# A hybrid decoder layer with routed experts: expert 1's low parts, the slot tables and the finishing of places, moved

## The chip, the cores and the metric

The kernel runs on one core of one Trainium2 chip. The metric is the device time of one execution in microseconds (us); of a kernel the median over its runs is given.

## The reference

Sixteen learned rows are put ahead of 2048 tokens of width 1024, and one decoder layer is computed: a projection, a pooling mixer and gated linear attention, an output projection added to the input, a router, and sixteen experts of which each token visits two. The last step is a final norm. What matters here is the router and the experts:

```python
def hier_moe(x, w_rg, b_rg, w_re, b_re, w_gate, w_up, w_down):
    ...
    g_sel = jnp.argmax(g_logits, axis=-1)
    p_g = jnp.take_along_axis(g_prob, g_sel[:, None], axis=-1)
    ...
    top_p, top_i = lax.top_k(e_prob, TOP_K_IN_GROUP)
    top_p = top_p / jnp.sum(top_p, axis=-1, keepdims=True)
    weights = p_g * top_p
    expert_id = g_sel[:, None] * EXPERTS_PER_GROUP + top_i
    combine = jnp.sum(jax.nn.one_hot(expert_id, N_EXPERTS, dtype=f32) * weights[..., None], axis=1)
    y = jnp.zeros(xf.shape, f32)
    for e in range(N_EXPERTS):
        h = jax.nn.silu(xt @ w_gate[e]) * (xt @ w_up[e])
        y = y + combine[:, e:e + 1] * (h @ w_down[e]).astype(f32)
```

Everything is float32; an expert has 256 hidden columns.

## The kernel before, in words

Tokens go in 16 tiles of 128 rows. Every float32 product is made of three matmuls, high by high, low by high and high by low, so each operand is split: ScalarE writes the rounded high part (L111 for weights, L107 for tokens), and VectorE or GpSimd the rest as the low part (L112, L108).

**Routing.** `route_pick` (L583) finds the two experts of each token of a tile and writes a 0/1 matrix `A` (L615). `route_rest` (from L620) turns it into slots: tiny matmuls with a matrix of ones (`ones_b`) and a triangular one (`before_b`) count the tokens that came before (L645, L647), VectorE computes slot numbers from the counts (L662 to L676, `ix` is the result), and GpSimd writes a record per token and expert into the table in HBM through an indirect DMA (L690). For the last tile two more tiny matmuls (L641, L642) and an addition (L643) give the total of each expert. `rank_experts` (L708) sorts the experts by their totals.

**Places.** The sixteen experts are then worked off in sixteen places; the first two places hold experts 0 and 1, the others hold experts by rank. A place has up to 320 slots, in row groups j = 0, 1, 2 of 128, 128 and 64 rows (the last six places only 0 and 1). For a place the kernel loads the slot table's columns into SBUF (`load_places`, L1105, by SyncE), sets the words of tokens' first and second visit (`fix_words`, seven VectorE operations, L1115 to L1121), gathers the tokens' rows (`xg`, `xs`, indirect DMAs of GpSimd, all in the helper on L924), transposes them on TensorE (L946) with the split behind it (L107 on ScalarE, L108 on VectorE), and does the gate and up products. For places 0 and 1 these are `gate_rows` (L995 to L997, one row group at a time, since routing isn't finished when they start); later `gate_up` (L975 to L977). Then come `hidden`, the down products (`down`, L1036 to L1041), and their evacuation with the routing weight (L1052 on ScalarE, L1054 on VectorE) into a row tile `xr`, of which six form a ring.

**What a token's two visits need.** A place scatters its rows into a buffer `oe` in HBM, then gathers from `oe` what an earlier place has left for its tokens, adding it (`xr<-oe`). `square` (L1072, ScalarE) sums the squares, and `finish` scales the finished rows (L1078, three operations for three row groups) and scatters them into the output (`out_dram<-xr`). `finish(e-1)` stands behind `down(e)` for most places, so these scatters follow place e's scatters and gathers on GpSimd's queue.

**Weights.** Chunks of 128x1024 come through SyncE into buffers `raw` (three) and `wr` (two), in order; a buffer is free when both halves of its split are done. Expert 1's four chunks (`wb` 0 to 3) are split while the last tile is routed, with their low parts on GpSimd.

**What sets the order.** A tile scheduler places instructions by priority and dependence when the program is built; each engine then runs its own in that order. `must_follow` adds an order that the data don't ask for. Around the change these are: the counts of the last tile behind a given matmul of expert 0's `gate_rows` (`picked`, `gate_ops`), and expert 1's splits. Rows of TensorE are in this order: expert 0's row groups 0 and 2, expert 1's row groups 0 and 2 (banks `sp` and `o`), expert 0's and 1's row group 1, whose tokens are known only after routing.

Of the kernel before, what the change touches and what calls it, by code (L numbers as in the profile page):

```python
# [12 lines left out]
OP = mybir.AluOpType  # L13
# [4 lines left out]
NT = 16  # L18
# [52 lines left out]
def body(ctx, tc, I, O):  # L71
# [16 lines left out]
    def must_follow(ins, earlier):  # L88
        for o_ in earlier:
            tc.add_manual_dep(ins.ins, o_.ins.name,  # L90
                              mybir.DependencyInfo(mybir.DependencyClass.Sync, mybir.DependencyReason.DATA),
                              reason="rows written through indices")
# [527 lines left out]
    def route_rest(t):  # L620

        T = lambda n, w, dt=F32: wk.tile([128, w], dt, name=n)
        lg, r, gm, m1, m2, Ef, A, xn = OUT.pop(t)
        i = t - 1
        rc = rec[t % 3]
        rf = rc.bitcast(F32)
        sv = sv_all[:, i, :]
        first = t <= EARLY
        pp = bank("m2", (128, 2, 16))
        if t == EARLY + 1:  # L630
            nc.tensor.matmul(pp[:, 1], ones_b, acc[i % 2], start=True, stop=True)
            early = pp[:, 1]
            V.tensor_copy(counts, early)
            for row, at in ((late1, 128.0), (late2, float(SMALL)), (late3, float(CAP))):
                V.tensor_scalar(row[:, FIXED:], early[:, FIXED:], -1.0, at, op0=OP.mult, op1=OP.add)
            V.tensor_scalar(late2[:, :FIXED], early[:, :FIXED], -1.0, float(CAP), op0=OP.mult, op1=OP.add)
            V.tensor_scalar(late2[:, :FIXED], late2[:, :FIXED], 128.0, None, op0=OP.min)
            V.tensor_copy(late3[:, :FIXED], late2[:, :FIXED])
            V.scalar_tensor_tensor(late0[:, FIXED:], early[:, FIXED:], 48.0, iota16[:, FIXED:], op0=OP.mult, op1=OP.add)
        elif t == NT:  # L640
            nc.tensor.matmul(pp[:, 1], ones_b, acc[i % 2], start=True, stop=False)  # L641
            nc.tensor.matmul(pp[:, 1], ones_b, A, start=False, stop=True)  # L642
            V.tensor_tensor(counts, pp[:, 1], counts, op=OP.add)  # L643
        pp = pp[:, 0]
        picked[0] = nc.tensor.matmul(pp, before_b, A, start=True, stop=(t == EARLY + 1))  # L645
        if t != EARLY + 1:
            nc.tensor.matmul(pp, ones_b, acc[i % 2], start=False, stop=True)  # L647
        ngm, eg, sg, nm1, p2, den, w = T("ngm", 1), T("eg", 4), T("sg", 1), T("nm1", 1), T("p2", 1), T("den", 1), T("w", 2)
        V.tensor_scalar(ngm, gm, -1.0, None, op0=OP.mult)
        nc.scalar.activation(eg, lg[:, 0:4], AF.Exp, bias=ngm, accum_out=sg)  # L650
        V.tensor_scalar(nm1, m1, -1.0, None, op0=OP.mult)
        nc.scalar.activation(p2, m2, AF.Exp, bias=nm1)
        v16, t1, t2, tmp, vv = T("v16", 16), T("t1", 16), T("t2", 16), T("tmp", 16), T("vv", 2)
        lev = T("lev", 16)
        if first:
            V.scalar_tensor_tensor(v16, pp, 48.0, iota16, op0=OP.mult, op1=OP.add)
            V.scalar_tensor_tensor(t1, pp, 128.0, step1, op0=OP.is_ge, op1=OP.mult)
            V.tensor_tensor(lev, pp, from2, op=OP.is_ge)
            V.tensor_tensor(t2, lev, step2, op=OP.mult)
            V.scalar_tensor_tensor(lev, pp, float(CAP), lev, op0=OP.is_ge, op1=OP.add)  # L660
        else:
            V.tensor_tensor(v16, pp, per_slot, op=OP.mult)  # L662
            V.tensor_tensor(v16, v16, late0, op=OP.add)
            V.tensor_tensor(t1, pp, late1, op=OP.is_ge)
            V.tensor_tensor(t1, t1, step1, op=OP.mult)
            V.tensor_tensor(lev, pp, late2, op=OP.is_ge)
            V.tensor_tensor(t2, lev, late_step2, op=OP.mult)
            V.tensor_tensor(tmp, pp, late3, op=OP.is_ge)
            V.tensor_tensor(lev, lev, tmp, op=OP.add)
        V.tensor_add(v16, v16, t1)  # L670
        V.tensor_add(v16, v16, t2)
        for j in range(2):
            V.scalar_tensor_tensor(tmp, Ef[:, j], 1.0, v16, op0=OP.mult, op1=OP.mult, accum_out=vv[:, j:j + 1])
            V.scalar_tensor_tensor(tmp, Ef[:, j], 1.0, iota16, op0=OP.mult, op1=OP.mult, accum_out=sv[:, j:j + 1])
        ix = T("ix", 2, I32)
        last = V.tensor_copy(ix, vv)  # L676
        V.scalar_tensor_tensor(den, p2, 1.0, sg, op0=OP.add, op1=OP.mult)
        V.reciprocal(w[:, 0:1], den)
        V.tensor_mul(w[:, 1:2], w[:, 0:1], p2)
        tok = tok_all[:, i:i + 1]  # L680
        V.tensor_copy(rc[:, :, 0], tok.to_broadcast([128, 2]))
        V.tensor_scalar(rf[:, :, 6], tok.to_broadcast([128, 2]), OOB, None, op0=OP.add)
        for j in range(2):
            V.tensor_copy(rf[:, j, 5:6], sv[:, 1 - j:2 - j])
        V.tensor_scalar(rf[:, :, 3], w, r, None, op0=OP.mult)
        r2 = T("r2", 1)
        V.tensor_mul(r2, r, r)
        V.tensor_scalar(rf[:, :, 4], r2.to_broadcast([128, 2]), EPS * SCALE, None, op0=OP.mult)
        for j in range(2):
            s_ = nc.gpsimd.indirect_dma_start(  # L690
                out=table, out_offset=bass.IndirectOffsetOnAxis(ap=ix[:, j:j + 1], axis=0),
                in_=rc[:, j, :], in_offset=None, bounds_check=6143, oob_is_err=False)
            for o_ in table_ops:
                tc.declare_no_dep(s_.ins, o_.ins, reason="other slots")
            table_ops.append(s_)
        oe_ops.append((-1, nc.gpsimd.dma_start(oe[i * 128:t * 128, :], xn)))
        if t == EARLY + 1:
            V.tensor_copy(acc[(i + 1) % 2], A)
        elif t < NT:
            V.tensor_tensor(acc[(i + 1) % 2], acc[i % 2], A, op=OP.add)  # L700
        V.tensor_copy(sv[:, 2:4], w)
        for j in range(2):
            V.scalar_tensor_tensor(tmp, Ef[:, j], 1.0, lev, op0=OP.mult, op1=OP.mult, accum_out=sv[:, 4 + 3 * j:5 + 3 * j])  # L703
        V.tensor_copy(sv[:, 5:6], rf[:, 0, 4:5])
        V.tensor_copy(sv[:, 6:7], r)
        return last
# [197 lines left out]
    with ExitStack() as c2:  # L904
# [230 lines left out]
            for k in range(KB):  # L1135
                transposes(0, k, (0, 2), added[0])
        early = [gate_rows(0, 0, "mm"), gate_rows(0, 2, "mm", lambda k: k < 6 or transposes(1, k - 6, (0, 2)))]
        must_follow(picked[0], [gate_ops[2]])
        for k in range(4):
            split_chunk(nc.gpsimd)  # L1140
            load_chunks(min(8 + k, 10))
        for k in range(2, KB):
            transposes(1, k, (0, 2))
        load_places(0, FIXED, slice(0, FIXED))
        fix_words(0, FIXED, iota16)
        for e in range(FIXED, NE):
            load_places(e, e + 1, expert(e))
        first_rows = [ind(XG[e][1], hn_dram, col(e, 1, 0), False) for e in range(2)]
        gather(2)
# [15 lines left out]
                    transposes(0, i, (1,))  # L1165

        early_1 = [gate_rows(1, 0, "sp"), gate_rows(1, 2, "o", early_rest)]
        down(0, (0, 2))
        for e in range(NE):
            def between(i):  # L1170
                if e + 1 < NE and i % 2 == 0:
                    for k in range(i, i + 2):
                        transposes(e + 1, k, None if e else (1,))
                if e == 0:
                    if i in (2, 6):
                        fix_words(*((2, 9) if i == 2 else (9, 16)), place)
                    if i == 0:
                        for op in load_chunks(10 + WRB, mk):
                            must_follow(op, first_rows)
                else:  # L1180
                    if done[0] < len(stream) and (i < 2 if e == NE - 1 else i in (0, 1, 2, 3, 4, 6)):
                        gate = stream[done[0]][0] == "g"
                        for op in split_chunk():
                            if gate:
                                must_follow(op, hidden_done)
                        load_chunks(done[0] + WRB, mk)
                if e >= NE - 2 and i == 1:
                    RT[e] = [row_tile(True) for j in JS[e]]
                    for j in JS[e]:
                        add_oe(e, ind(RT[e][j][:rows[j]], oe, col(e, j, 0), False), True)  # L1190
# [16 lines left out]
            if e > 1:  # L1207
                for j in JS[e - 1]:
                    square(e - 1, j)
            if e == NE - 2:  # L1210
                finish(e - 1)
            down(e, None if e else (1,))
            if 1 < e < NE - 2:
                finish(e - 1)
            if e == 8:
                count_left(mk)

# [132 lines left out]
```

## Time and profile before

| what | value |
|---|---|
| median of 3 runs | 1127.05 us (1126.39 to 1127.88) |
| the profiled execution's own time | 1121.29 us |
| its span, first to last instruction | 1119.5 us |
| mean granted TensorE clock | 0.982 |
| TensorE busy | 1055.8 us, 94% |
| VectorE busy | 779.8 us, 70% |
| ScalarE busy | 565.7 us, 51% |
| GpSimd busy | 313.8 us, 28% |

Rows name an engine (PE is TensorE, DVE VectorE, ACT ScalarE, POOL GpSimd, SP SyncE), a line of the kernel, the operation and the tiles it writes and reads. In brackets stands how long the engine had been idle and what it waited for last. The clock is a share of TensorE's full rate.

### The profile page before, as it was taken

Reading aid. Unit: us, or ns where it says so; the run is one execution under the profiler, and the core shown is the slowest. Engines: PE = TensorE matmul, PEld = TensorE weight load, DVE = VectorE, ACT = ScalarE, POOL = GpSimd, SP = SyncE. Lnnn points to the kernel's source line nnn. Section 1 sums busy time; section 2 is a strip of 40 time slices with the busy share of each in tenths; the row PEclk is TensorE's granted clock in tenths of the full one; section 3 lists DMA queues with packets and bytes.
Section 4 is the critical chain, followed back from the end, with each engine's and each line's share of the span. In section 5 each row is a group of like instructions: output and inputs, shape, how many; then the busy total and the mean of one; then the engine's idle time right before and its main releaser. Section 6 shows DMA issues by size and latency. Waiting matters only on the chain. (4 is left out here: it accounts for less than half of the span.)

```text
span 1119.5 us, 19115 instructions
## 1 busy us (share of the span) xinstructions
PE 1055.8 (94%) x6614; PEld 946.5 (85%) x6614; DVE 779.8 (70%) x2649; ACT 565.7 (51%) x1192; POOL 313.8 (28%) x276
## 2 busy tenths in 40 slices
PE   7999999999999999999999998879999999989982
PEld 5888888888888889999999998558998899988861
DVE  6476666545555776878777788747787788867873
ACT  7545444334433643333333334337767777667741
POOL 2000000000000000121111105524677777776551
PEclk9999999999999999999999999989999999989996
DMA  8412332111121352533434344488888997889852
GB/s 279 166 66 76 107 101 90 62 57 48 67 85 57 115 196 67 170 142 120 145 124 151 114 153 160 132 235 237 221 248 230 242 264 214 231 256 311 255 152 74
DMA packets 64471, 174.09 MB, mean 156 GB/s; under 512 B 21012, under 2 KB 21317, under 8 KB 64368
## 3 DMA queue, kind: packets, MB, share of 16 engines
q1 hardware_dynamic: 36272, 105.72, 27.7%
q0 software_dynamic: 25504, 58.53, 20.0%
q10 hardware_dynamic: 2592, 8.55, 2.1%
q8 instruction: 54, 0.88, 0.3%
q14 instruction: 49, 0.40, 0.1%
HBM read 143.74 MB, written 57.74 MB: 180 GB/s over the span
## 5 line engine op out<-in xcount | busy, mean ns | idle before, releaser
L441 POOL DMA_DIRECT2D y_dram<-y x16 | 8.6, 541 | 391.2 <-DVE y L439 391.2
L924 POOL DMA_INDIRECT oe<-xr,tab x40 | 69.3, 1732 | 69.0 <-ACT xr L1052 57.3
L321 PE MATMUL mm<-wb,XL 128*128 128x512 f32 (+1 forms) x240 | 83.6, 348 | 0.0
L322 PE MATMUL mm<-wb,XH 128*128 128x512 f32 (+1 forms) x240 | 83.0, 346 | 0.0
L690 POOL DMA_INDIRECT table<-rec,ix x32 | 33.3, 1042 | 176.8 <-DVE tmp L703 85.4
L320 PE MATMUL mm<-wb,XH 128*128 128x512 f32 (+1 forms) x240 | 82.2, 342 | 0.0
L924 POOL DMA_INDIRECT xr<-oe,tab x39 | 75.4, 1932 | 17.8 <-issue 9.8
L523 PE MATMUL mm<-XL,ws 128*128 128x256 f32 (+1 forms) x256 | 73.0, 285 | 0.2 <-DVE XL L112 0.2
L522 PE MATMUL mm<-XH,ws 128*128 128x256 f32 (+1 forms) x256 | 73.0, 286 | 0.0
L524 PE MATMUL mm<-XH,ws 128*128 128x256 f32 (+1 forms) x256 | 72.2, 282 | 0.0
L111 ACT ACTIVATE XH<-xt 128x1024 fp32r<-128x1024 f32 x32 | 33.8, 1058 | 56.4 <-PE mm L524 36.0
L924 POOL DMA_INDIRECT out_dram<-xr,tab x39 | 55.6, 1426 | 20.8 <-DVE sr_y L60 7.4
L975 PE MATMUL mm<-xh,ws 128*128 128x320 f32 (+1 forms) x168 | 51.3, 306 | 0.0
L976 PE MATMUL mm<-xl,ws 128*128 128x320 f32 (+1 forms) x168 | 51.2, 305 | 0.0
L977 PE MATMUL mm<-xh,ws 128*128 128x320 f32 (+1 forms) x168 | 51.0, 304 | 0.0
L320 PE MATMUL mm<-ws,XH 128*128 128x512 f32 x112 | 47.4, 423 | 2.0 <-ACT XH L111 2.0
L321 PEld LDWEIGHTS mm<-wb,XL 128*128 128x128 f32 x240 | 45.4, 189 | 4.4
L1078 DVE SCALAR_TENSOR_TENSOR xr<-xr,sr_y,fw 128x1024 f32<-128x1024 f32 (+1 forms) x39 | 48.7, 1278 | 0.5
L320 PEld LDWEIGHTS mm<-wb,XH 128*128 128x128 f32 x240 | 45.1, 188 | 4.6
L322 PEld LDWEIGHTS mm<-wb,XH 128*128 128x128 f32 x240 | 45.1, 188 | 4.5
L523 PEld LDWEIGHTS mm<-XL,ws 128*128 128x128 f32 x256 | 48.1, 188 | 0.7 <-DVE XL L112 0.4
L524 PEld LDWEIGHTS mm<-XH,ws 128*128 128x128 f32 x256 | 48.4, 189 | 0.3 <-issue 0.2
(654 smaller groups left out, 3840.8 us busy)
## 6 DMA issues: line engine op xcount, KB each, us to landing
raw<-in_wgu_e_dram SPq DMA_DIRECT2D x42, 512.0 KB, 5.2
xt<-in_xT_dram SPq DMA_DIRECT2D x32, 512.0 KB, 3.5
xn<-in_xn_dram SPq DMA_DIRECT2D x32, 512.0 KB, 3.5
wr<-in_wgu_e_dram SPq DMA_DIRECT2D x22, 512.0 KB, 5.9
raw<-in_wd_e_dram SPq DMA_DIRECT2D x20, 512.0 KB, 5.6
hn_dram<-xn ACTq DMA_DIRECT2D x16, 512.0 KB, 3.3
oe<-xn POOLq DMA_DIRECT2D x16, 512.0 KB, 3.7
wr<-in_wd_e_dram SPq DMA_DIRECT2D x12, 512.0 KB, 5.8
```

What stands on the lines that cost most here:

```text
L111: return (nc.scalar.activation(hi, src, AF.Copy), (eng or V).tensor_tensor(lo, src, hi.bitcast(F32), op=OP.subtract))
L320: nc.tensor.matmul(q, xh[:, k, :], wh[:, c0:c1_], start=(k == 0), stop=False)
L321: nc.tensor.matmul(q, xl[:, k, :], wh[:, c0:c1_], start=False, stop=False)
L322: nc.tensor.matmul(q, xh[:, k, :], wl[:, c0:c1_], start=False, stop=(k == KB - 1))
L522: nc.tensor.matmul(ps[:, b], WS[k][0][:, c], XH[:, k, o:], start=(k == 0), stop=False)
L523: nc.tensor.matmul(ps[:, b], WS[k][0][:, c], XL[:, k, o:], start=False, stop=False)
L524: nc.tensor.matmul(ps[:, b], WS[k][1][:, c], XH[:, k, o:], start=False, stop=(k == KB - 1))
L924: return nc.gpsimd.indirect_dma_start(out=out_, out_offset=off if scatter else None, in_=in_, in_offset=None if scatter else off, bounds_c ...
L975: nc.tensor.matmul(p[:, c0:c1_], wh, xh, start=(k == 0), stop=False)
L976: nc.tensor.matmul(p[:, c0:c1_], wh, xl, start=False, stop=False)
L977: nc.tensor.matmul(p[:, c0:c1_], wl, xh, start=False, stop=(k == KB - 1))
L1078: V.scalar_tensor_tensor(x[:n], x[:n], r[:n], fw[:n], op0=OP.mult, op1=OP.mult)
```

## The change

Four things are changed.

1. For the last tile, `route_rest` puts the two `before_b`/`ones_b` matmuls first and the two that make the totals behind them; all four now follow the matmul of k = 6 of expert 0's row group 2 instead of k = 2.
2. The low parts of expert 1's four chunks go from GpSimd to VectorE, and each must follow the cast to `ix` of the last tile.
3. Of the table loads, those of places 0 to 4 remain ahead of the first gathers; those of 5 to 8 are made in place 0's products and those of 9 to 15 in place 1's. The fix of places 0 and 1 stands behind expert 1's early rows, that of places 2 to 8 goes from place 0's products to place 1's, that of 9 to 15 from place 0's to place 2's.
4. `finish(e-1)` stands ahead of `down(e)` for all places, where it stood behind it for places 2 to 13.

```diff
--- before.py
+++ after.py
@@ -637,14 +637,14 @@
             V.tensor_scalar(late2[:, :FIXED], late2[:, :FIXED], 128.0, None, op0=OP.min)
             V.tensor_copy(late3[:, :FIXED], late2[:, :FIXED])
             V.scalar_tensor_tensor(late0[:, FIXED:], early[:, FIXED:], 48.0, iota16[:, FIXED:], op0=OP.mult, op1=OP.add)
-        elif t == NT:
-            nc.tensor.matmul(pp[:, 1], ones_b, acc[i % 2], start=True, stop=False)
-            nc.tensor.matmul(pp[:, 1], ones_b, A, start=False, stop=True)
-            V.tensor_tensor(counts, pp[:, 1], counts, op=OP.add)
-        pp = pp[:, 0]
+        total, pp = pp[:, 1], pp[:, 0]
         picked[0] = nc.tensor.matmul(pp, before_b, A, start=True, stop=(t == EARLY + 1))
         if t != EARLY + 1:
             nc.tensor.matmul(pp, ones_b, acc[i % 2], start=False, stop=True)
+        if t == NT:
+            nc.tensor.matmul(total, ones_b, acc[i % 2], start=True, stop=False)
+            nc.tensor.matmul(total, ones_b, A, start=False, stop=True)
+            V.tensor_tensor(counts, total, counts, op=OP.add)
         ngm, eg, sg, nm1, p2, den, w = T("ngm", 1), T("eg", 4), T("sg", 1), T("nm1", 1), T("p2", 1), T("den", 1), T("w", 2)
         V.tensor_scalar(ngm, gm, -1.0, None, op0=OP.mult)
         nc.scalar.activation(eg, lg[:, 0:4], AF.Exp, bias=ngm, accum_out=sg)
@@ -1135,15 +1135,14 @@
             for k in range(KB):
                 transposes(0, k, (0, 2), added[0])
         early = [gate_rows(0, 0, "mm"), gate_rows(0, 2, "mm", lambda k: k < 6 or transposes(1, k - 6, (0, 2)))]
-        must_follow(picked[0], [gate_ops[2]])
+        must_follow(picked[0], [gate_ops[6]])
         for k in range(4):
-            split_chunk(nc.gpsimd)
+            must_follow(split_chunk()[1], [routed])
             load_chunks(min(8 + k, 10))
         for k in range(2, KB):
             transposes(1, k, (0, 2))
         load_places(0, FIXED, slice(0, FIXED))
-        fix_words(0, FIXED, iota16)
-        for e in range(FIXED, NE):
+        for e in range(FIXED, 5):
             load_places(e, e + 1, expert(e))
         first_rows = [ind(XG[e][1], hn_dram, col(e, 1, 0), False) for e in range(2)]
         gather(2)
@@ -1165,15 +1164,19 @@
                     transposes(0, i, (1,))
 
         early_1 = [gate_rows(1, 0, "sp"), gate_rows(1, 2, "o", early_rest)]
+        fix_words(0, FIXED, iota16)
         down(0, (0, 2))
         for e in range(NE):
             def between(i):
                 if e + 1 < NE and i % 2 == 0:
                     for k in range(i, i + 2):
                         transposes(e + 1, k, None if e else (1,))
+                later = 5 + i if e == 0 and i < 4 else 9 + i if e == 1 and i < 7 else 0
+                if later:
+                    load_places(later, later + 1, expert(later))
+                if e in (1, 2) and i == 2:
+                    fix_words(*((2, 9) if e == 1 else (9, 16)), place)
                 if e == 0:
-                    if i in (2, 6):
-                        fix_words(*((2, 9) if i == 2 else (9, 16)), place)
                     if i == 0:
                         for op in load_chunks(10 + WRB, mk):
                             must_follow(op, first_rows)
@@ -1207,11 +1210,8 @@
             if e > 1:
                 for j in JS[e - 1]:
                     square(e - 1, j)
-            if e == NE - 2:
                 finish(e - 1)
             down(e, None if e else (1,))
-            if 1 < e < NE - 2:
-                finish(e - 1)
             if e == 8:
                 count_left(mk)
```

How instructions move, at three places. First TensorE at the last tile's counts (`m` is the bank of the counts, `mm` expert 0's gate rows; the first matmul of totals, L641, stands further ahead, in row group 0). Before:

```order
L996 MATMUL mm<-ws_78,xl_8621 64x512
L997 MATMUL mm<-ws_79,xh_8620 64x512
L642 LDWEIGHTS ones_b
L642 MATMUL m_8533<-A,ones_b 128x16
L995 MATMUL mm<-ws_80,xh_8620 64x512
L996 MATMUL mm<-ws_80,xl_8621 64x512
L997 MATMUL mm<-ws_81,xh_8620 64x512
L645 LDWEIGHTS before_b
L645 MATMUL m_8533<-A,before_b 128x16
L647 LDWEIGHTS ones_b
L647 MATMUL m_8533<-acc_188,ones_b 128x16
L995 MATMUL mm<-ws_80,xh_8620 64x512
```

and now, with the lines of the changed kernel (L641 and L643 are the counts before a token, L645 and L646 the totals):

```order
L995 MATMUL mm<-ws_84,xh_8620 64x512
L996 MATMUL mm<-ws_84,xl_8621 64x512
L997 MATMUL mm<-ws_85,xh_8620 64x512
L641 LDWEIGHTS before_b
L641 MATMUL m_8533<-A,before_b 128x16
L643 LDWEIGHTS ones_b
L643 MATMUL m_8533<-acc_188,ones_b 128x16
L645 LDWEIGHTS ones_b
L645 MATMUL m_8533<-acc_188,ones_b 128x16
L646 LDWEIGHTS ones_b
L646 MATMUL m_8533<-A,ones_b 128x16
```

`A` is now read fifteen gate-row matmuls later than its first reader was, and no tiny matmul stands ahead of it.

Second VectorE, behind the last tile's `ix` (`wb_87`, `wb_89` and `wb_91` are low parts of expert 1's first three chunks):

```order
+L112 TENSOR_TENSOR wb_87<-raw,wb_86 128x1024
+L724 TENSOR_REDUCE t_8604<-sq 128x14
+L112 TENSOR_TENSOR wb_89<-raw,wb_88 128x1024
+L725 CAST expert_at<-t_8604 128x14
+L112 TENSOR_TENSOR wb_91<-raw,wb_90 128x1024
 L108 SCALAR_TENSOR_TENSOR wb_99<-tp,vecs,wb_98 128x192
-L724 TENSOR_REDUCE t_8604<-sq 128x14
```

The three low parts now stand on this queue, among the last steps of ranking. Further on, in expert 1's early rows (`xl_8621` are low parts of expert 0's row group 1, `L1115` with 128x336 is the first operation of the fix of places 2 to 8; the whole fix leaves this stretch):

```order
 L112 TENSOR_TENSOR HB<-tp,HB 128x2x64
-L1115 TENSOR_TENSOR sq<-tab,iota_114 128x336
 L108 SCALAR_TENSOR_TENSOR xl_8621<-zg,vecs,xh_8620 128x128
-L108 SCALAR_TENSOR_TENSOR xl_8621<-tp,vecs,xh_8620 128x128
-L1116 TENSOR_TENSOR sq<-sq,place 128x336
-L108 SCALAR_TENSOR_TENSOR xl_8621<-zg,vecs,xh_8620 128x128
-L1117 TENSOR_REDUCE sq<-sq 128x21
-L108 SCALAR_TENSOR_TENSOR xl_8621<-tp,vecs,xh_8620 128x128
-L1118 TENSOR_TENSOR sq<-sq,iota_114 128x21
-L108 SCALAR_TENSOR_TENSOR xl_8621<-zg,vecs,xh_8620 128x128
-L1119 SCALAR_TENSOR_TENSOR tab<-sq,tab 128x3x7
-L1120 TENSOR_SCALAR sq<-sq 128x21
```

The splits no longer stand between the steps of the fix.

Third GpSimd's queue in a place with three row groups (buffer numbers 9275 to 9277 are the rows of place 2, 9543 to 9545 and 9570 to 9572 those of place 3, 9865 to 9867 those of place 4). Before, the end of place 3:

```order
L924 DMA xr_9544<-oe_164,tab_155 128x1024
L924 DMA oe_164<-xr_9545,tab_155 2048x1024
L924 DMA xr_9545<-oe_164,tab_155 64x1024
L924 DMA out_0_dram<-xr_9275,tab_155 2048x1024
L924 DMA out_0_dram<-xr_9276,tab_155 2048x1024
L924 DMA out_0_dram<-xr_9277,tab_155 2048x1024
```

and now, in place 4:

```order
L924 DMA oe_164<-xr_9865,tab_155 2048x1024
L924 DMA xr_9865<-oe_164,tab_155 128x1024
L924 DMA out_0_dram<-xr_9570,tab_155 2048x1024
L924 DMA out_0_dram<-xr_9571,tab_155 2048x1024
L924 DMA out_0_dram<-xr_9572,tab_155 2048x1024
L924 DMA oe_164<-xr_9866,tab_155 2048x1024
L924 DMA xr_9866<-oe_164,tab_155 128x1024
L924 DMA oe_164<-xr_9867,tab_155 2048x1024
L924 DMA xr_9867<-oe_164,tab_155 64x1024
```

The three output scatters of the place before stand between the first row group's pair and the second's, where they stood behind the third's.

## Rows read from the trace of the kernel before

**Rows 1.** The page's first section, busy time by engine, share of the span, instructions.

```profile
PE 1055.8 (94%) x6614; PEld 946.5 (85%) x6614; DVE 779.8 (70%) x2649; ACT 565.7 (51%) x1192; POOL 313.8 (28%) x276
```

**Rows 2.** PE's timeline, 700 to 710 us: start, duration, instruction, [idle before <-releaser].

```profile
700.36 0.17 PE L641 MATMUL m<-acc,ones_b 128*128 128x16 bf16 x1 [2.71 <-DVE tmp L668]
...
705.58 0.39 PE L997 MATMUL mm<-ws,xh 128*64 128x512 f32 x1
708.67 0.17 PE L642 MATMUL m<-A,ones_b 128*128 128x16 bf16 x1 [2.70 <-DVE A L615]
```

**Rows 3.** PE's timeline, 726 to 740 us.

```profile
726.76 0.27 PE L946 MATMUL zg<-ident,xg 128*128 128x128 f32 x1
...
735.34 0.47 PE L946 MATMUL zg<-ident,xg 128*128 128x128 f32 x1 [7.04 <-DVE xl L108]
```

**Rows 4.** Busy PE by stretch: us, busy (instructions), granted clock, DMA share, GB/s.

```profile
709.75:713.10 3.35, 3.35 (x9) 0.51 0.02 5
735.34:739.10 3.76, 3.76 (x12) 0.50 0.54 151
```

**Rows 5.** POOL's timeline, 695 to 717 us.

```profile
695.47 7.08 POOL L112 TENSOR_TENSOR wb<-raw,wb 128x1024 fp32r<-128x1024 f32 x3 [6.59 <-PE ds L572]
...
714.03 1.03 POOL L690 DMA_INDIRECT table<-rec,ix  x1 [2.81 <-DVE sq L721]
715.36 1.76 POOL L690 DMA_INDIRECT table<-rec,ix  x1 [0.30 <-DVE t L724]
```

**Rows 6.** DVE's timeline, 700 to 717 us.

```profile
700.23 2.35 DVE L667 TENSOR_TENSOR t<-lev,late_step 128x16 f32<-128x16 f32 x1
...
711.60 0.16 DVE L665 TENSOR_TENSOR t<-t,step 128x16 f32<-128x16 f32 x1
...
713.58 0.16 DVE L676 CAST ix<-vv 128x2 int32<-128x2 f32 x1
...
715.04 1.22 DVE L112 TENSOR_TENSOR wb<-raw,wb 128x1024 fp32r<-128x1024 f32 x1
```

**Rows 7.** DVE's timeline, 732 to 741 us.

```profile
734.51 0.51 DVE L1115 TENSOR_TENSOR sq<-tab,iota 128x336 f32<-128x336 f32 x1 [7.33 <-DMA tab<-table]
```

**Rows 8.** SP's timeline, 715 to 736 us.

```profile
718.34 17.05 SPq L1105 DMA_DIRECT2D tab<-table  x15
```

**Rows 9.** DMA issues of 690 to 780 us: count, size, median us to landing.

```profile
raw<-in_wgu_e_dram SPq DMA_DIRECT2D x7, 512.0 KB, 6.4
raw<-in_wd_e_dram SPq DMA_DIRECT2D x4, 512.0 KB, 4.2
...
tab<-table SPq DMA_DIRECT2D x14, 12.0 KB, 5.3
```

**Rows 10.** POOL's timeline, 846 to 872 us, place 4.

```profile
846.48 1.59 POOL L924 DMA_INDIRECT oe<-xr,tab  x1 [1.49 <-ACT xr L1052]
...
857.21 3.37 POOL L924 DMA_INDIRECT xr<-oe,tab  x1 [0.30 <-issue]
...
865.84 0.96 POOL L924 DMA_INDIRECT xs<-hn_dram,tab  x1 [0.30 <-issue]
```

**Rows 11.** ACT's timeline, 860 to 875 us.

```profile
869.07 1.04 ACT L1072 ACTIVATE sq<-xr 64x1024 bf16<-64x1024 f32 x1
```

**Rows 12.** PE's waits of 780 to 1000 us: us in total, times, longest.

```profile
PE tp L946 <- ACT xr L1052: 4.0, 1, 4.0
PE zg L946 <- DVE xr L1054: 1.8, 6, 0.3
```

**Rows 13.** The page's costliest groups: busy, mean ns.

```profile
L1078 DVE SCALAR_TENSOR_TENSOR xr<-xr,sr_y,fw 128x1024 f32<-128x1024 f32 (+1 forms) x39 | 48.7, 1278 | 0.5
```

**Rows 14.** DMA issues of 800 to 1000 us.

```profile
xr<-oe,tab POOLq DMA_INDIRECT x26, 6.0
```

**Rows 15.** ACT's timeline, 980 to 1000 us.

```profile
990.14 0.69 ACT L1052 ACTIVATE xr<-sp,tab 128x512 f32<-128x512 f32 x1 [4.24 <-DMA out_dram<-xr,tab]
```

**Rows 16.** POOL's timeline, 1057 to 1105 us.

```profile
1075.17 1.00 POOL L924 DMA_INDIRECT xr<-oe,tab  x1 [3.63 <-DMA xr<-oe,tab]
```

## The prediction, made before the changed kernel was run

> **What bounds the kernel now.** I began with the busy time by engine: TensorE is busy 94% of the span [rows 1], so time can only come from its idle stretches, from stretches at the lower clock, or from less work, and the change removes no matmul. TensorE's timeline around the end of routing shows the idle stretches. A matmul of totals waits 2.71 us for VectorE's L668, the next waits 2.70 us for `A` [rows 2], and, while expert 1's early rows run, a transpose waits 7.04 us for a low part on VectorE [rows 3]: 12.45 us together. After the second and after the third the granted clock is 0.51 and 0.50, the lower of the two levels (1.2 GHz), in stretches of 3.35 and 3.76 us in which TensorE is never idle [rows 4]. At 2.4 GHz the same matmuls would take half, so these cost 1.6 and 1.9 us more.
>
> Then what each wait stands on. VectorE's small operations are stretched while GpSimd works through three low parts, 7.08 us from 695.47 [rows 5]: L667 takes 2.35 us there, while its like L665 takes 0.16 when GpSimd is quiet [rows 6]. The 7.04 us have another cause. VectorE stood 7.33 us at the first operation of the fix of places 2 to 8, for a table load [rows 7], and the split that TensorE needed is behind it on the same queue. The loads are slow because SyncE issues fifteen in a row, over 17.05 us [rows 8].
>
> **The change part by part.**
>
> Counts and low parts. Between the two idle times TensorE runs 23 matmuls, from 700.39 to 705.97 [rows 2], 0.243 us each. Without the first idle time it ends them at 703.3; fifteen more and two transposes, and it reaches the four tiny matmuls at about 707.1. `A`, which released a matmul at 708.67 [rows 2], comes at least 2.19 us earlier when L667 alone shrinks to 0.16 [rows 6], so by 706.5: both early waits go, with the lower clock behind them. That is 5.41 + 1.6 = 7.0 us.
>
> What is late next: the low parts must follow `ix`. From L665 to `ix` it took 2.0 us [rows 6], with four such operations ahead 2.4; from 707.1 and 0.3 for the counts to land, `ix` comes at 709.8 instead of 713.58. The first low part starts about 0.9 us behind it and takes 1.22 [rows 6], so it is there at 711.9. TensorE, with 7 matmuls and 6 transposes between the counts and its first reader, gets there at 709.5: a new wait of 2.4. The first splits also free the buffers for chunks 7 to 9. Landing costs between 4.2 and 6.4 us [rows 9]; I take 4.2, since the fifteen table loads that crowded the queues are not yet issued. Chunk 7 then lands at 716.1, chunk 9 at about 718.7; its low part, 1.22, and a high part that I put at the same length bring the last at about 721, and VectorE's last token splits stand behind it. I take 1.0 us of wait there (0 to 3.2, the upper end with 6.4 for landing). GpSimd loses four instructions and issues its table writes at once.
>
> The fix leaves the early rows: 7.04 + 1.9 = 8.9 us off. What is late next is the gather of expert 0's row group 1. From `ix` to its first transpose it took 726.76 - 713.58 = 13.2 us [rows 3, 6]; from 709.8 that is 723.0, and TensorE wants it just ahead of the down products, which began at 739.1, the end of the second stretch in [rows 4], and will begin some 12.5 us sooner, so at about 725: covered, by 2 us.
>
> So to the first down products of place 0: -7.0 - 8.9 + 2.4 + 1.0 = **-12.5 us**.
>
> The fixes, later. Seven operations, the longest half a microsecond [rows 7], now stand among splits in places 1 and 2. The loads of places 5 to 9 are issued behind five weight chunks, some 10 us ahead of their fix, and take 5.3 to land [rows 9]. Between 0 and 2 us; I take **+0.5**, since VectorE is not the bound there.
>
> Finish ahead of down. Three scalings of 1.28 [rows 13] now stand ahead of the last evacuations on VectorE, where TensorE already waits six times 0.3 us in a cycle [rows 12]. But TensorE's transposes that need those banks were moved some sixteen matmuls on too, which at 320 columns instead of 512 is 16 x 0.243 x 320/512 = 2.4 us. Between 0 and 1.4 a place (3.8 less 2.4), eight places; nearest to those 0.3 us waits, I take 0.12 each, **+1.0**. On GpSimd three output scatters, from 860.88 to 865.84 [rows 10], 4.96 us, go ahead of the second and third row groups. The third gather goes out at 857.21 - 846.48 = 10.7 us after the place's first scatter [rows 10]; it will be 15.7. With 6.0 us to land [rows 14] the rows are there at 21.7, and `square` of that row group runs at 869.07 - 846.48 = 22.6 [rows 11]: covered, with 0.9 us to spare, so 0. At place 9 the output scatters go out sooner, so of the 4.24 us that ScalarE waits for a row tile there [rows 15] a little goes; but now the squares of the same place wait for their later gathers instead, some 0.4 us sooner: **-0.4**. At the end two output scatters, two thirds of 4.96, go ahead of place 13's second scatter, behind which the gathers of place 14 wait. GpSimd idles 3.63 us there for a DMA already [rows 16], which covers a part: 0 to 3.3, I take **+1.0**.
>
> Sum: -12.5 + 0.5 + 1.0 - 0.4 + 1.0 = -10.4. From the profiled execution's 1121.29 that is 1110.9; the median shown lies 5.76 above it, so 1127.05 - 10.4 = **1116.6 us**.
>
> A rule weighed. A table write on GpSimd took 1.03 us alone and the next 1.76, partly beside a low part on VectorE [rows 5, 6], so such a neighbour may cost a GpSimd DMA 0.7 us. The Trainium skill, SBUF — State Buffer, section "Who interferes with whom", says that a VectorE instruction with two SBUF inputs and a GpSimd one that reads SBUF lock each other out for a whole instruction, but infers that `tensor_tensor` doesn't starve descriptor writing. By its first half each write could stand behind whole low parts; by its inference, nothing.
>
> **The rivals.**
>
> *The writes are held.* If the last table writes wait out the three low parts now beside them, 3 x 1.22 us, the gather lands at 726.7 and not at 723.0, and the 2 us of cover are short by 1.7: 1118.3. The 1.76 us speaks for a part of it, the 0.9 us overlap against all. This is the page's rule from the paragraph above, as a mechanism here.
>
> *Place 9's wait goes too.* If the earlier scatters free the row tile wholly, TensorE's 4.0 us wait for ScalarE [rows 12] goes, and with it, if the clock fell there as behind the 7.04 us, 1.9 us more: -5.9 for -0.4, 1111.1. For it: ScalarE waits for an output scatter there. Against it: the later squares.
>
> *The squares bind a little.* If the third gather lands 8.0 us after issue instead of 6.0, ScalarE waits 1.1 us in each of seven cycles, and evacuation, on which TensorE waits already, passes it on: +7.7, 1124.3; half of that, 1120.5.
>
> *Slower.* The same queue with more crowding: if it lands after half as long again and a little, 9.1 us, each of the seven places is 2.2 us longer, and VectorE's 1.4 us of uncovered scaling in some of them adds to it: +15.4 and more, 1132. It decides for slower from 1.8 us a cycle, a landing of 8.7 us. For it: a DMA can take that long where GpSimd's gather itself takes 3.37 us [rows 10]. Against it: 6.0 is a median of 26.
>
> *Nothing comes of it.* The early 12.5 us are given back, if weights, not TensorE, then set the pace of the places: 1127. Against it: 94% busy [rows 1].
>
> **How the numbers follow.** Forecast 0.58 (own range 1113 to 1120.5, from the bounds above); writes held 0.07; place 9 0.13; squares 0.10; slower 0.07; nothing 0.05. The range leaves out slower, nothing, and the far ends of squares and place 9: 1108 to 1123. About 0.2%, 2.25 us, can be told from no change. Faster: 0.58 + 0.07 + 0.13 + 0.10 = 0.88; same 0.05; slower 0.07.
>
> **What would show it.** Right: no TensorE idle time at the tiny matmuls; one of about 2.4 us at the first L997 of bank `sp`; no wait of the early transposes for a fix; the first down products near 726.6 instead of 739.1; L663 to L667 of the last tiles at 0.16 us. Wrong: squares on ScalarE that wait for `xr<-oe`, places longer than before, TensorE waits at L946 of over 1 us in each place, or first down products later than 730.

## The result, and the profile after

| | median us | runs |
|---|---|---|
| before | 1126.72 | 4 (1122.58 to 1127.88) |
| after | 1142.68 | 4 (1142.48 to 1142.87) |

The ratio is 1.0148, with a 95% interval of 1.0122 to 1.0174: the change makes the kernel slower by 1.5%, some 16.7 us. The profiled execution after is one of 1142.64 us. The page of the changed kernel, its first section:

```profile
span 1140.9 us, 19115 instructions
...
PE 1061.5 (93%) x6614; PEld 951.8 (83%) x6614; DVE 777.5 (68%) x2653; ACT 567.1 (50%) x1192; POOL 306.9 (27%) x272
```

TensorE was busy for 94% of the span before [rows 1] and for 93% now. Where it stands idle, the view of its waits from 695 us to the end tells (us in total, times, longest):

```profile
PE tp L946 <- ACT xr L1052: 17.1, 10, 3.6
PE ds L1037 <- DVE HB L112: 10.5, 2, 8.6
PE zg L1007 <- DVE h L1004: 6.7, 1, 6.7
PE sp L997 <- DVE wb L112: 2.3, 1, 2.3
```

The first row is the wait of which [rows 12] have one piece of 4.0 us; before, it came to 5.3 us in two waits over the same stretch, and now it is ten waits and 17.1 us. The second row is new. The waits for the counts [rows 2] are gone, and the fourth row is the wait of 2.3 us for the first low part that was forecast.

**The early part.** The windows of TensorE after (busy us, granted clock, DMA share, GB/s):

```profile
720.00:740.00 20.00, 18.70 (x88) 1.00 0.86 240
740.00:760.00 20.00, 11.39 (x47) 0.74 0.72 214
760.00:780.00 20.00, 18.09 (x88) 0.91 0.77 228
```

From 720 to 740 us TensorE works nearly without a gap at the full clock; from 740 to 760 it is busy 11.39 us of 20 at 0.74. Three views of that stretch tell why. First SyncE's timeline (start, duration, instruction):

```profile
734.92 0.34 SPq L759 DMA_DIRECT2D raw<-in_wgu_e_dram  x1
735.79 13.51 SPq L1105 DMA_DIRECT2D tab<-table  x4
```

Four table loads, behind five weight chunks, occupy SyncE for 13.51 us, from the first one's start to the last one's end; before, fifteen took 17.05 [rows 8]. Then VectorE's:

```profile
753.07 0.51 DVE L1115 TENSOR_TENSOR sq<-tab,iota 128x336 f32<-128x336 f32 x1 [8.68 <-DMA tab<-table]
753.50 0.42 DVE L112 TENSOR_TENSOR HB<-zg,HB 128x256 fp32r<-128x256 f32 x1
```

The first operation of the fix of places 2 to 8 waits 8.68 us for such a load. Right behind it on the queue stands the low part of place 0's last hidden rows. And TensorE's:

```profile
753.97 0.80 PE L1037 MATMUL ds<-wb,HB 128*128 128x512 f32 x1 [8.61 <-DVE HB L112]
754.57 0.63 PE L1038 MATMUL ds<-wb,HB 128*128 128x512 f32 x1
```

That low part is what TensorE waits 8.61 us for. Behind the wait a matmul takes 0.63 us; the granted clock is 0.50 from 753.97 to 758.40 us, the lower level (1.2 GHz), as in [rows 4]. This is the wait of 7.04 us [rows 3, 7], some twenty microseconds further on.

What the fix waits for is the landing of the loads, and not only SyncE's slow issue. The tables' words move in packets under 512 B. Of all DMA packets these are the counts from 736 to 748 us and from 748 to 753 us:

```profile
DMA packets 1076, 3.90 MB, mean 325 GB/s; under 512 B 126, under 2 KB 126, under 8 KB 1075
...
DMA packets 1879, 0.99 MB, mean 198 GB/s; under 512 B 1649, under 2 KB 1649, under 8 KB 1879
```

Two of the four loads were issued before 738 us, but nearly all small packets move after 748 us, behind the weights that stand ahead of them in SyncE's queue.

**The places.** GpSimd's timeline in place 4:

```profile
854.45 1.60 POOL L924 DMA_INDIRECT oe<-xr,tab  x1 [3.12 <-ACT xr L1052]
...
858.93 1.53 POOL L924 DMA_INDIRECT out_dram<-xr,tab  x1 [0.31 <-issue]
...
870.95 1.81 POOL L924 DMA_INDIRECT xr<-oe,tab  x1 [0.30 <-issue]
...
880.74 1.61 POOL L924 DMA_INDIRECT oe<-xr,tab  x1 [3.08 <-ACT xr L1052]
```

From the first scatter to the third gather it is now 870.95 - 854.45 = 16.5 us, where it was 10.7 [rows 10]; the three output scatters stand in between, from 858.93 on. The next place's first scatter is at 880.74, 26.3 us after this place's. Before, it was 24.6 us after it (846.48 in [rows 10]):

```profile
871.05 1.60 POOL L924 DMA_INDIRECT oe<-xr,tab  x1 [1.36 <-ACT xr L1052]
```

ScalarE's timeline there, after:

```profile
878.74 1.06 ACT L1072 ACTIVATE sq<-xr 64x1024 bf16<-64x1024 f32 x1 [1.59 <-DMA xr<-oe,tab]
```

The square of the third row group waits 1.59 us for the gather and starts 24.3 us after the first scatter; before it started at 22.6 [rows 10, 11] and waited for no DMA.

One thing in this trace is not of the change. Some 20 us ahead of the counts a transpose waits 3.44 us; the second line is the wait for the first low part (PE's timeline):

```profile
690.09 0.35 PE L946 MATMUL tp<-ident,xs 128*128 128x128 f32 x1 [3.44 <-DVE tmp L703]
...
715.94 0.50 PE L997 MATMUL sp<-wb,wb 128*128 128x512 f32 x1 [2.25 <-DVE wb L112]
```

In run 1 below (finish behind down), the same program up to there, this wait is 1.1 us and `ix` comes 5.7 us earlier (708.04 against 713.79). So this trace runs some 5 us late from there on. Of the other runs with parts 1 and 2, run 11 alone waits as long there (3.45 us; the others 0.8 to 1.5). The cause of this wait stays open, and so does whether the other executions of the changed kernel have it. It is not what makes the loss: run 3 waits 1.6 us there and loses 14.9 us by part 4 alone.

### The profile page after: what moved, and what is told of

It is laid out like the page before. It is cut to its first block, busy times and chain, and to the rows that moved or that the text cites. A ratio compares the mean times of both kernels' runs of the same rounds, so it can differ in the third digit from the quotient of the medians.

```text
span 1140.9 us, 19115 instructions
## 1 busy us (share of the span) xinstructions
PE 1061.5 (93%) x6614; PEld 951.8 (83%) x6614; DVE 777.5 (68%) x2653; ACT 567.1 (50%) x1192; POOL 306.9 (27%) x272
## 5 line engine op out<-in xcount | busy, mean ns | idle before, releaser
L112 DVE TENSOR_TENSOR wb<-raw,wb 128x1024 fp32r<-128x1024 f32 x39 | 47.5, 1219 | 8.8 <-ACT wb L111 7.8
```

The lines of the kernel that those rows point to most:

```text
L112: (eng or V).tensor_tensor(lo, src, hi.bitcast(F32), op=OP.subtract))
```

## The experiments

Ratios are to the kernel before, timed in the same session, with their 95% intervals. The theory "squares" says that the output scatters ahead of the second and third row groups cost the places their time; "tables" that late table loads do.

**1. Finish behind down.**

```diff
+            if e == NE - 2:
                 finish(e - 1)
             down(e, None if e else (1,))
+            if 1 < e < NE - 2:
+                finish(e - 1)
```

> The changed kernel with finish(e-1) behind down(e) again for places 2 to 13; the other three parts stay. Theory 'squares' (the three output scatters ahead of the second and third row groups' gathers make ScalarE's square of the third row group wait, and the evacuation and TensorE with it): TensorE's 17 us of waits for L1052 shrink to about 5, 1125 to 1129 us. Rival 'tables' (the late table loads and the wait for the fix in place 0 cost the time): 1139 to 1143, and places of over 26 us stay. Rival 'pace' (weights set the pace of the places whatever is done ahead of them): 1139 to 1143.

Measured 1125.45 us against 1122.84, ratio 1.0028 (1.0013 to 1.0044). TensorE's waits:

```profile
PE ds L1037 <- DVE HB L112: 12.6, 2, 9.3
PE tp L946 <- ACT xr L1052: 5.7, 2, 3.9
```

The waits for the evacuation are back at 5.7 us, but the 12.6 us for the hidden low part stay. So part 4 costs 1.0148 / 1.0028, 1.2%, and the other three parts together gain nothing. This trace tells the landing of the late table loads, too. The first two, which SyncE issued in 1.63 us, landed 16.4 us after their issue (median), all four 9.3 to 16.9 us after it:

```profile
tab<-table SPq DMA_DIRECT2D x2, 12.0 KB, 16.4
```

**2. Tables and fixes early.**

```diff
-        for e in range(FIXED, 5):
+        fix_words(0, FIXED, iota16)
+        for e in range(FIXED, NE):
             load_places(e, e + 1, expert(e))
...
-                if e in (1, 2) and i == 2:
-                    fix_words(*((2, 9) if e == 1 else (9, 16)), place)
+                    if i in (2, 6):
+                        fix_words(*((2, 9) if i == 2 else (9, 16)), place)
```

> The changed kernel with all fifteen table loads ahead of the first gathers and the fixes where they were before; low parts on VectorE, the counts and finish ahead of down stay. Theory 'squares': the 8.6 us wait in place 0 goes, but the 7 us wait of the early transposes comes back, and places stay at 26 us: 1139 to 1144. Rival 'tables': the slowdown goes, 1124 to 1130.

Measured 1129.46 against 1122.84, ratio 1.0062 (1.0038 to 1.0086). Both theories missed: 7 us above before, between the two. Undoing part 3 alone takes away 0.9% (1.0148 / 1.0062), so "squares" alone is not the cause, nor is "tables". There are two, of like size.

**3. Finish ahead, alone.** The kernel before with part 4.

```diff
-            if e == NE - 2:
                 finish(e - 1)
             down(e, None if e else (1,))
-            if 1 < e < NE - 2:
-                finish(e - 1)
```

> The kernel before with one part of the change, finish(e-1) ahead of down(e) for all places. Theory 'squares': 1140 to 1145, with squares that wait 1 to 3 us in each place from 4 to 9. Rivals 'tables' and 'pace': 1125 to 1129.

Measured 1137.74 against 1122.84, ratio 1.0137 (1.0112 to 1.0163), 14.9 us. ScalarE's waits from 775 to 1060 us:

```profile
ACT sq L1072 <- DMA xr<-oe,tab: 16.8, 12, 3.2
```

A dozen squares wait 16.8 us, without any of the other parts. The gathers of 800 to 1000 us land later than in [rows 14], where the median was 6.0:

```profile
xr<-oe,tab POOLq DMA_INDIRECT x24, 7.7
```

"Squares" holds for this part of the loss.

**4. Scalings ahead, scatters held.**

```diff
...
                 finish(e - 1)
             down(e, None if e else (1,))
+            if 1 < e < NE - 2:
+                for j in JS[e - 1]:
+                    must_follow(store(e - 1, j, RT[e - 1][j]), [oe_ops[-1][1]])
```

(`scale_out` no longer stores for those places.)

> The changed kernel, but of finish only the scalings stand ahead of down(e); the output scatters must follow the place's third gather, as in the kernel before. It tells GpSimd's order from VectorE's. Theory 'squares': GpSimd's order alone costs the time, so 1125 to 1130, as without the move. Rival 'scalings' (three scalings of 1.28 us ahead of VectorE's evacuations lengthen each place by the 1.5 us): 1138 to 1144, with squares that no longer wait.

Measured 1135.45 against 1122.84, ratio 1.0123 (1.0097 to 1.0149). That reads as "scalings", but it is a fault of the experiment. ScalarE's waits:

```profile
ACT xr L1052 <- DMA out_dram<-xr,tab: 11.8, 6, 7.0
```

No square waits any more. But my ordering made the scatters wait until the gather had landed, row tiles came free later, and the ring of six ran out. Run 5 mends it.

**5. Scatters behind in the queue's order alone.**

```diff
-                    must_follow(store(e - 1, j, RT[e - 1][j]), [oe_ops[-1][1]])
+                    queued_after(store(e - 1, j, RT[e - 1][j]), oe_ops[-1][1])
```

> The run with the scalings ahead of down and the scatters behind, again, but with the scatters behind the third gather only in GpSimd's order, not behind its landing: in that run ScalarE waited 11.8 us for row tiles whose scatters had been held. Theory 'squares': as the run with all of finish behind down, 1 to 5 us slower than the kernel before. Rival 'scalings': 10 us slower or more.

Measured 1126.69 against 1122.75, ratio 1.0026 (1.0012 to 1.0040), as run 1. ScalarE's waits:

```profile
ACT sq L1072 <- DVE HB L961: 5.2, 8, 0.8
...
ACT xr L1052 <- DMA out_dram<-xr,tab: 3.9, 1, 3.9
```

Scalings ahead of down cost nothing that shows; GpSimd's order is the whole of part 4's loss.

**6. Parts 1 and 2 alone.** The kernel before with the change's hunk in `route_rest` and

```diff
-        must_follow(picked[0], [gate_ops[2]])
+        must_follow(picked[0], [gate_ops[6]])
         for k in range(4):
-            split_chunk(nc.gpsimd)
+            must_follow(split_chunk()[1], [routed])
```

> The kernel before with parts 1 and 2 of the change alone (counts together behind k = 6, expert 1's low parts on VectorE); tables, fixes and finish as before. In the run with the tables early, place 1's down products began 9 us sooner than in the kernel before. Theory 'parts add up' (that lead is kept once finish stays behind down): 7 to 11 us faster than the kernel before. Rival 'pace' (weights set the pace, so the lead is given back): within 2 us of the kernel before.

Measured 1114.02 against 1122.75, ratio 0.9923 (0.9907 to 0.9939): 8.7 us faster. "Pace" falls. And from here to run 1, part 3 costs 1.0028 / 0.9923, 1.06%, some 12 us. VectorE's timeline has the first operation of the fix of places 2 to 8 where it stood before:

```profile
728.64 0.51 DVE L1115 TENSOR_TENSOR sq<-tab,iota 128x336 f32<-128x336 f32 x1 [1.80 <-DMA tab<-table]
```

It waits 1.80 us for a table load instead of 7.33 [rows 7], though the fix has not been moved.

**7. Low parts alone.**

```diff
-            split_chunk(nc.gpsimd)
+            must_follow(split_chunk()[1], [routed])
```

> The kernel before with part 2 alone: expert 1's low parts on VectorE behind the last ix; the counts stay behind k = 2. If GpSimd beside VectorE caused both early waits, the first (2.71 us) goes and the second keeps only what TensorE needs to wait for A: 5 to 9 us faster than the kernel before, most of what parts 1 and 2 give together. If the order of the counts caused them: within 3 us of the kernel before.

Measured 1118.97 against 1127.15, ratio 0.9923 (0.9899 to 0.9947), all that the two parts give together. VectorE's timeline, two operations of the tile before the last, and the last tile's `ix`:

```profile
699.20 0.17 DVE L663 TENSOR_TENSOR v<-v,late 128x16 f32<-128x16 f32 x1
...
699.37 0.16 DVE L665 TENSOR_TENSOR t<-t,step 128x16 f32<-128x16 f32 x1
...
709.35 0.16 DVE L676 CAST ix<-vv 128x2 int32<-128x2 f32 x1
```

TensorE's waits of 695 to 722 us:

```profile
PE m L642 <- DVE A L615: 0.3, 1, 0.3
```

**8. Counts alone.** The kernel before with the change's hunk in `route_rest` and

```diff
-        must_follow(picked[0], [gate_ops[2]])
+        must_follow(picked[0], [gate_ops[6]])
```

> The kernel before with part 1 alone: the four tiny matmuls together behind k = 6, low parts on GpSimd. If GpSimd's low parts are the cause of the waits: L663, L665 and L667 still take 1 to 2.3 us, TensorE no longer waits for them at the counts, but ix comes later; 0 to 5 us faster than the kernel before. If the order is the cause: 6 to 9 us faster, as parts 1 and 2 together.

Measured 1124.18 against 1127.15, ratio 0.9973 (0.9957 to 0.9989). VectorE's timeline:

```profile
698.03 1.34 DVE L663 TENSOR_TENSOR v<-v,late 128x16 f32<-128x16 f32 x1
...
699.38 2.35 DVE L665 TENSOR_TENSOR t<-t,step 128x16 f32<-128x16 f32 x1
...
715.80 0.16 DVE L676 CAST ix<-vv 128x2 int32<-128x2 f32 x1
```

TensorE's waits of 695 to 722 us:

```profile
PE m L641 <- DVE A L615: 2.1, 1, 2.1
```

With GpSimd beside them, the same two operations (L663 and L665 of the tile before the last) take 1.34 and 2.35 us, as L667 in [rows 6], and the last `ix` is at 715.80; in run 7, with GpSimd's low parts gone, they take 0.17 and 0.16, and `ix` is at 709.35. At the counts TensorE waits 0.3 us in run 7 and still 2.1 us for `A` in run 8, in spite of the counts' later place. GpSimd's low parts were the cause of the early waits; the order of the counts adds little (0.27% alone, nothing that shows beside part 2).

**9. Fixes one place later**, with the late loads and finish behind down.

```diff
...
-                if e in (1, 2) and i == 2:
-                    fix_words(*((2, 9) if e == 1 else (9, 16)), place)
+                if e in (2, 3) and i == 2:
+                    fix_words(*((2, 9) if e == 2 else (9, 16)), place, hidden_done[0])
```

(The new argument keeps the first operation behind the hidden split on VectorE's queue.)

> The run with finish behind down, but the two fixes stand behind place 1's and place 2's hidden split on VectorE, so that no split that TensorE needs stands behind them; the late table loads stay. Theory 'fix waits' (TensorE's 9.3 and 3.2 us waits behind VectorE's fix, and the lower clock after them, are all that late tables cost): 8 to 14 us faster than the kernel before. Rival 'held queue' (SyncE's two long issues also hold the weights behind them): the waits reappear at ScalarE's high parts of the weights, within 4 us of the kernel before.

Measured 1112.87 against 1122.75, ratio 0.9913 (0.9895 to 0.9930), 9.9 us faster than before, and 1.15% below run 1. SyncE's timeline and TensorE's wait for token low parts in this run:

```profile
715.14 5.37 SPq L1105 DMA_DIRECT2D tab<-table  x5
726.87 0.34 SPq L1152 DMA_DIRECT2D fw<-in_fnw_dram  x1
727.46 0.35 SPq L759 DMA_DIRECT2D raw<-in_wgu_e_dram  x1
...
731.26 14.61 SPq L1105 DMA_DIRECT2D tab<-table  x4
```

```profile
PE zg L946 <- DVE xl L108: 2.6, 2, 1.6
```

The four table loads still take 14.61 us, but TensorE's waits at L1037 for the hidden low part, 12.6 us in run 1, are gone. What late loads cost was the fix that stood ahead of a needed low part. Against run 6 (0.9923, 0.9907 to 0.9939) the intervals overlap, so it is not shown that part 3 gains anything even with the fixes out of the way.

**10. Tables early, fixes late.** Run 6 (all loads ahead) with the fixes as in run 9.

```diff
-                    if i in (2, 6):
-                        fix_words(*((2, 9) if i == 2 else (9, 16)), place)
...
+                if e in (2, 3) and i == 2:
+                    fix_words(*((2, 9) if e == 2 else (9, 16)), place, hidden_done[0])
```

> Parts 1 and 2, all table loads ahead as in the kernel before, finish behind down as in the kernel before, and the two fixes one place later as in the run above. Both theories: faster than the run with parts 1 and 2 alone by the 1.5 us wait of an early transpose and what goes with it, 9 to 14 us faster than the kernel before. If the fixes cost nothing where they stood, no different from parts 1 and 2 alone.

Measured 1117.84 against 1122.75, ratio 0.9952 (0.9935 to 0.9968): slower than parts 1 and 2 alone, which neither theory expected. SyncE's timeline and ScalarE's:

```profile
715.10 16.44 SPq L1105 DMA_DIRECT2D tab<-table  x15
...
732.71 0.35 SPq L759 DMA_DIRECT2D raw<-in_wgu_e_dram  x1
```

```profile
742.52 1.06 ACT L111 ACTIVATE ws<-raw 128x1024 fp32r<-128x1024 f32 x1 [2.82 <-DMA raw<-in_wgu_e_dram]
745.61 1.06 ACT L111 ACTIVATE wb<-wr 128x1024 fp32r<-128x1024 f32 x1 [2.03 <-DMA wr<-in_wd_e_dram]
```

The fifteen loads hold SyncE for 16.44 us, so the first weight chunk is issued at 732.71, 5 us later than in run 9, and ScalarE waits for the weights. With the fixes late, then, late loads are better than early ones, by 0.4% and with intervals that only just part. That does not explain why this run is slower than run 6, which issues its first chunk at 731.84, 0.9 us earlier, with all loads ahead as well; this stays open.

**11. Table loads in SyncE's pause.** Run 9, with the loads of places 5 to 8 ahead again.

```diff
-        for e in range(FIXED, 5):
+        for e in range(FIXED, 9):
...
-                later = 5 + i if e == 0 and i < 4 else 9 + i if e == 1 and i < 7 else 0
+                later = 9 + i if e == 1 and i < 7 else 0
```

> The run with the fixes one place later, but the loads of places 5 to 8 stand ahead of the first gathers again, in the 6.2 us in which SyncE otherwise waits for those gathers (from 720.7 to 726.9 in that run); those of 9 to 15 stay in place 1. Theory 'queue' (table loads cost where they stand behind or ahead of weight chunks, and nothing in the pause): SyncE's issues of 4 to 5 us are gone, the first weight chunk is issued within 1 us of that run's 727.5, and the time is 0 to 4 us below that run, 10 to 14 us faster than the kernel before. Rival 'number' (each table load ahead of the weights delays them by its 1.04 us): weights 4 us later, 5 to 9 us faster than the kernel before, as with all tables early.

Measured 1115.98 against 1127.15, ratio 0.9894 (0.9874 to 0.9915): 11 to 12 us faster than the kernel before, in the range of theory 'queue' and beyond that of 'number'. SyncE's timeline:

```profile
720.05 8.48 SPq L1105 DMA_DIRECT2D tab<-table  x8
...
732.42 0.69 SPq L759 DMA_DIRECT2D raw<-in_wgu_e_dram  x1
...
736.57 0.56 SPq L1105 DMA_DIRECT2D tab<-table  x1
```

Eight loads take 8.48 us and end ahead of the gathers that SyncE waits for anyway; no load is held. This trace is some 5 us late in the early part like that of the change, so times are told from the first wait at L997 on (716.35 here, 711.45 in run 9): the first weight chunk is issued 16.1 us behind it here and 16.0 there. The interval overlaps run 9's and run 6's, so whether it is better than those is not settled; all three beat the kernel before and the change.

## Why the prediction was wrong

Forecast was 1116.6 us, 0.88 for faster; measured is 1142.68. Two steps failed, both by the time that a DMA takes to land. By the terms of the sum:

- **Counts and low parts, -7.0, +2.4 and +1.0.** Right in mechanism: both early waits go, the 2.4 us wait for the first low part came as 2.25, and without this trace's late start `ix` came at 708.0 to 709.4 in runs 1 and 7, forecast was 709.8. The first down products, forecast near 726.6, began at 728.5 after the change and at 723.3 in run 1, where they began at 739.1 before. The size was too small: the terms make -3.6, and parts 1 and 2 alone gave -8.7 (run 6). The rival that table writes are held found no support: the two last writes took 1.00 and 1.20 us beside the low parts in the trace after.
- **The fix leaves the early rows, -8.9.** The wait left the early rows, but came back as one of 8.6 us in place 0's down products. The term was also booked to the wrong part: in run 6, where the fix stays and only `ix` comes earlier, its wait has already shrunk from 7.33 to 1.80 us, so moving it had little left to gain. The reading that these loads "are slow because SyncE issues fifteen in a row" was incomplete: the last load that this fix needs is place 8's, issued at 726.3 as the eighth of them, and it took 8.0 us to land.
- **The fixes, later, +0.5.** This step failed. It said that the loads of places 5 to 9 (5 to 8 in the code) are issued "some 10 us ahead of their fix, and take 5.3 to land". After the change the fix was ready at 744.4 us; the first two loads had been issued 8.6 and 7.5 us ahead of that, the last, held on SyncE, only 0.7. But behind five weight chunks all four took 9.3 to 16.9 us to land (run 1), those that SyncE issued at once the longest, and the fix waited 8.68 us. I had taken the landing from the median of loads that stood in a row of their own, and had priced seven short operations, but not the wait of the first, which holds what is behind it on VectorE, though [rows 7] showed just that. Part 3 costs some 12 us by runs 1 and 6, and 0.9%, some 10 us, by run 2.
- **Finish ahead of down, scatters: 0.** This step failed too. The third gather goes out after 16.5 us, where 15.7 were forecast, and lands by 24.3, 7.8 later, where I took the median of 6.0; 22.6 was the limit. Both errors go the same way and the margin was 0.9. The median was the wrong figure even before any crowding: the very gather of [rows 10], issued at 857.21 in the kernel before, took 8.1 us to land, which went unseen, since its square came 3.8 us after that. Part 4 costs 13.5 to 15 us by runs 1 and 3, close to the 15.4 of the rival "slower", which had this mechanism and a chance of 0.07. That rival asked for 9.1 us to land; 7.8 was enough, with the gather issued 0.8 later than forecast and a wait of 3.39 us at place 9 beside the 1.6 of place 4.
- **Scalings ahead, +1.0.** Run 5 is level with run 1, so nothing shows; right within its bounds.
- **Place 9, -0.4, and the end, +1.0.** In the changed kernel the wait for an output scatter at place 9 is gone, and the squares wait 3.39 us there for a gather instead, as said. At the end TensorE's wait at L1007 grew from 3.0 to 6.7 us, by 3.7 where 3.3 was my bound. That is part 4's doing: the wait is 7.3 us in run 3, with part 4 alone, and 3.9 in run 1, without it.

These are the two landings in the kernel before, the load of place 8 and the third gather of place 4 (DMA issues of 726.4 to 726.8 us and of 857.15 to 857.3 us):

```profile
tab<-table SPq DMA_DIRECT2D x1, 12.0 KB, 8.0
...
xr<-oe,tab POOLq DMA_INDIRECT x1, 8.1
```

By runs 6, 1 and the change the parts are -0.77%, +1.06% and +1.20%; that these make +1.5% follows from how they are worked out. A test that does not is run 2, which has parts 1, 2 and 4: run 6 times run 3 gives 0.9923 x 1.0137 = 1.0059, and run 2 measured 1.0062.

## What to carry to other kernels

An operation that waits for a late DMA costs what stands behind it on its queue, so it is to be placed by what follows it, not by when its result is needed. When work is put ahead on an in-order queue, everything behind it moves by the whole of it: compare that with the margin of the first reader, and take the landing time of that very transfer, under the load of that stretch and with its spread, not the median of many. Two parts of one change that hide each other's effect are only seen when each is taken out alone, and then put in alone.

## What the runs showed of the hardware

Small operations of VectorE with two operands in SBUF take 0.17 us, and 1.3 to 2.35 us beside a 128x1024 subtraction on GpSimd that takes 2.4; with one operand in PSUM they kept 0.16. GpSimd's last two table writes took 1.00 and 1.20 us beside VectorE's own subtractions of this size, where one alone took 1.03 [rows 5]; the 1.76 us of the other in [rows 5] did not come again. The Trainium skill, SBUF — State Buffer, section "Who interferes with whom", tells of a probe in which `tensor_tensor` on VectorE did not stall DMA, and infers that it leaves GpSimd the port that descriptor writing needs. This trace agrees, to 0.2 us.

SyncE's issue of a small table load takes 0.54 us in a row of such loads, but single ones behind five chunks of 512 KB took up to 5.6 us after the change. Why an issue is held there, and from which number on, was not tried. Landing took 8.0 us for a load beside gathers in the kernel before, and 16.4 us for two loads behind five chunks in run 1.
